# Two buffers for the dense experts' gate tile, three instead of four for v's two parts

## The chip, the cores and the metric

One core of a Trainium2 chip runs the whole kernel. The metric is the device time of one execution in microseconds, the median over runs. TensorE (PE; its weight loads are PEld) does the matmuls, VectorE (DVE), ScalarE (ACT) and GpSimd (POOL) the rest, and SyncE (SP) issues most of the DMAs.

## What is computed

One block of an encoder on 1024 tokens of width 1024 in float32: a mixer (differential attention and a short convolution, gated and summed), then PEER, a retrieval over 128 x 128 experts of one neuron each, then a final norm. The change touches PEER alone:

```python
q = (xc @ w_query).reshape(c, PEER_HEADS, 2, PEER_HALF_DIM)
sc = jnp.einsum('chpd,hpnd->chpn', q, sub_keys)
s1, i1 = lax.top_k(sc[:, :, 0], PEER_TOPK); s2, i2 = lax.top_k(sc[:, :, 1], PEER_TOPK)
top, pos = lax.top_k(cand, PEER_TOPK)          # cand: sums of s1 and s2
g = jax.nn.softmax(top, axis=-1)
u = expert_u[eidx]
a = jax.nn.gelu(jnp.einsum('chkd,cd->chk', u, xc), approximate=False)
vv = expert_v[eidx]
out = jnp.einsum('chk,chkd->cd', g * a, vv)    # 8 heads x 16 experts of each token
```

## The kernel before, in words

The tokens are eight tiles of 128. The kernel computes PEER in two ways at once. For five tiles (640 tokens, "dense") it runs over all 16384 experts and multiplies by a gate that is zero for experts that were not chosen. For the other three tiles it gathers each token's 128 chosen experts from HBM.

**The dense part** (the loop at the end of `block_kernel`) takes the experts in 128 groups of 128; the text calls such a group an expert. `expert_in(i)` loads the group's rows of u (`raw`, three buffers, shared with v), splits them in two parts (`uh` by a cast on ACT, the remainder `uhl` on DVE), makes z = u h in 48 matmuls of 320 columns (two column halves, eight steps of K, three products of parts each), takes Gelu on ACT into `pr`, multiplies `pr` by the gates on DVE (line 930) and splits the product in `ph` and `phl`. `expert_v(i)` loads the rows of v and splits them in `vh` (ACT) and `vhl` (DVE), with `VHB` buffers of each. `expert_out` takes a block of two experts at once and adds their products to ten tiles of output (five token tiles, two halves of the width): four of them stay in PSUM (`held`), six go through `pout` and are added to `hacc` on DVE (line 957). Half of the ten tiles are done in each of two iterations, after `expert_in` and before `expert_v`. So both experts' `vh` and `vhl` are read until the second of these iterations is over; there are 30 matmuls of 512 columns in an iteration.

**The gates.** The weights of all experts for the dense tokens lie in HBM (`w_d`), written before this stage. Line 920 loads those of four experts at a time (`WB`) into `wt`, 1280 KB, in runs of 512 bytes, issued by SyncE; 32 such loads in all. Four multiplications of line 930 read one load. `wt`'s pool `dn` has room for one.

**The gathers** run beside it: POOL fetches one expert's u and v for each of 128 tokens by indirect DMA (1 MB, line 739) into `uvt` (four buffers); DVE takes the product with h (line 746), ACT Gelu and the gate (748, 749; this small tile is named `wt` as well), DVE adds v times that to `acc` (line 755). There are 384 of them. A generator hands out their instructions in step with the estimated time of the dense matmuls. The choice of experts for these tokens runs on DVE in the first part of the stage.

**Order.** The kernel is written in a tile language; buffers with the same tag rotate, and a tile waits until a buffer of its tag is free. The program is built with `tile.TileContext(nc, schedule_with_timeline_sim=True)`: the order of instructions on each engine is planned at build time along a simulated timeline and is then fixed, so it need not be the order of the code. Each engine, and SyncE's issuing, goes through its own list in order. A change of the number of buffers can change the plan.

Of the kernel before, what the change touches and what calls it, by code (L numbers as in the profile page):

```python
# [10 lines left out]
F32 = mybir.dt.float32  # L11
# [9 lines left out]
P = 128  # L21
# [6 lines left out]
GB = NB * P  # L28
# [15 lines left out]

UVT = 4
PHB = 4
VHB = 4
BLK = 2
NR = 2
WB = 4  # L50
WT = 32
# [14 lines left out]
def block_kernel(ctx, tc, x, wqkv, wcols, wpr, wo, wq, skT, uv, uT, an_w, fn_w, fin_w, sub_w,  # L66
# [7 lines left out]
    def pool(name, bufs=1, stack=None, **kw):  # L74
        return (stack or left).enter_context(tc.tile_pool(name=name, bufs=bufs, **kw))
# [382 lines left out]
    def halves(n):  # L458
        return [(0, n)] if n <= 512 else [(0, n // 2), (n // 2, n // 2)]
# [428 lines left out]
    du, dn, dv, hp, gat = (pool(n) for n in ("du", "dn", "dv", "hp", "gat"))  # L888
# [4 lines left out]
    def split(t, tag, bufs, shape, eng):  # L893
        pl = du if tag == "uh" else dv
        hi = pl.tile(shape, F32R, name=tag, tag=tag, bufs=bufs)
        A.copy(out=hi, in_=t)  # L896
        lo = pl.tile(shape, F32R, name=f"{tag}l", tag=f"{tag}l", bufs=bufs)
        eng.tensor_sub(lo, t, hi.bitcast(F32))  # L898
        return hi, lo

    def passes(ps, lhs, rhs, cols, first=True, last=True):
        n = len(lhs)
        for k in range(n):
            for j, (a, b) in enumerate(((0, 0), (0, 1), (1, 0))):
                PE.matmul(ps, lhsT=lhs[k][a], rhs=rhs[k][b],  # L905
                          start=first and k == 0 and j == 0, stop=last and k == n - 1 and j == 2)
        tick(cols / 2400 * 3 * n)

    wts = {}

    def raw_rows(src):
        t = du.tile([P, D], F32, name="raw", tag="raw", bufs=3)
        SP.dma_start(out=t, in_=src)
        return t

    def expert_in(i):
        b = i // WB
        if i % WB == 0:
            wts[b] = dn.tile([P, GB // WT, WB, WT], F32, name="wt", tag="wt", bufs=1)
            SP.dma_start(out=wts[b], in_=w_d[:, :, i:i + WB, :].rearrange("c p i t -> p c i t"))  # L920
        ur = raw_rows(uT[i])
        u = split(ur, "uh", 2, [P, D], V)
        us = [(u[0][:, k * P:(k + 1) * P], u[1][:, k * P:(k + 1) * P]) for k in range(KD)]
        hs = halves(GB)
        z = ps_z.tile([P, 2, 512], F32, name="z", tag="z")[:, :len(hs), :hs[0][1]]
        for j, (c0, cn) in enumerate(hs):
            passes(z[:, j, :], us, [(hh[:, k, c0:c0 + cn], hl[:, k, c0:c0 + cn]) for k in range(KD)], cn)
        p = dn.tile([P, GB], F32, name="pr", tag="pr", bufs=1)
        A.activation(p.rearrange("p (h c) -> p h c", h=len(hs)), z, AF.Gelu)  # L929
        V.tensor_mul(p.rearrange("p (c t) -> p c t", t=WT), p.rearrange("p (c t) -> p c t", t=WT),  # L930
                     wts[b][:, :, i % WB, :])
        return split(p, "ph", PHB, [P, GB], V)

    def expert_v(i):
        vr = raw_rows(uv[i * P:(i + 1) * P, D:])
        return split(vr, "vh", VHB, [P, D], V)

# [36 lines left out]
    for i in range(NK + BLK):  # L974
        if i < NK:
            pv.append(expert_in(i))
        b, part = i // BLK - 1, i % BLK
        if b >= 0:
            expert_out(pv[:BLK], vv[:BLK], part, b == 0, b == NK // BLK - 1)
            if part == BLK - 1:  # L980
                pv, vv = pv[BLK:], vv[BLK:]
        if i < NK:
            vv.append(expert_v(i))
        if i == 1:
            for t in range(NR, NB):
                SP.dma_start(out=hacc[:, t - NR, :], in_=h_d[t * P:(t + 1) * P, :])
# [56 lines left out]
```

## Time and profile before

| | |
|---|---|
| median of 3 runs | 3235.85 us (3223.81 to 3254.53) |
| the profiled execution | 3236.47 us, its span 3234.7 us |
| mean granted clock of TensorE over the span | 0.973 |
| dense stage | from about 1316 us to the end |

The profile is of one execution. A row of a stretch gives each engine's busy time and number of instructions, the granted clock as a share of full speed, the share of time that the 16 DMA engines were busy, and what they moved. A row of waits gives who waited, for whom, the sum in us, how often and the longest. A row of the timeline gives start and duration in us, the engine, line and operation, what is written and read, and in brackets how long the engine was idle before it and what ended that. Matmuls overlap in the pipeline, so their own durations are longer than their spacing.

### The profile page before, as it was taken

Reading aid. Unit: us, or ns where it says so; the run is one execution under the profiler, and the core shown is the slowest. Engines: PE = TensorE matmul, PEld = TensorE weight load, DVE = VectorE, ACT = ScalarE, POOL = GpSimd, SP = SyncE. Lnnn points to the kernel's source line nnn. Section 1 sums busy time; section 2 is a strip of 40 time slices with the busy share of each in tenths; the row PEclk is TensorE's granted clock in tenths of the full one; section 3 lists DMA queues with packets and bytes.
Section 4 is the critical chain, followed back from the end, with each engine's and each line's share of the span. In section 5 each row is a group of like instructions: output and inputs, shape, how many; then the busy total and the mean of one; then the engine's idle time right before and its main releaser. Section 6 shows DMA issues by size and latency. Waiting matters only on the chain.

```text
span 3234.7 us, 46047 instructions
## 1 busy us (share of the span) xinstructions
PE 3017.4 (93%) x17551; PEld 2768.1 (86%) x17551; DVE 2647.0 (82%) x4665; ACT 1298.3 (40%) x2344; POOL 954.6 (30%) x716
## 2 busy tenths in 40 slices
PE   7999999898999889799999999999999999999992
PEld 6799988798888779798989989889888999998891
DVE  4442565478999996798999999999999999998898
ACT  3322464335567757433333333333333333333332
POOL 2310000045444444232223323322333323233333
PEclk9999999999999989899999999999999999999996
DMA  5451232555444374787888888878789899988997
GB/s 177 146 177 66 82 111 92 211 164 202 146 177 182 148 269 161 265 297 274 304 291 293 308 286 315 323 275 316 268 301 339 325 348 338 339 329 317 327 331 288
DMA packets 237550, 801.12 MB, mean 248 GB/s; under 512 B 18832, under 2 KB 123280, under 8 KB 174096
## 3 DMA queue, kind: packets, MB, share of 16 engines
q0 software_dynamic: 64704, 442.53, 37.4%
q1 hardware_dynamic: 152592, 305.30, 27.2%
q10 hardware_dynamic: 20032, 50.34, 4.1%
q8 instruction: 138, 2.26, 0.3%
q14 instruction: 84, 0.69, 0.1%
HBM read 714.74 MB, written 83.36 MB: 247 GB/s over the span
## 4 chain that ended last, share of the span: by engine, by line
PE 36%; DVE 20%; issue 18%; DMA 15%; POOL 7%; ACT 3%; SPq 0%; POOLq 0%; ACTq 0%; DVEq 0%
DMA wt<-w_d 7%; PE z L905 7%; POOL uvt L739 6%; PE pg L228 4%; DMA uvt<-in_uv,idx 4%; PE pq L228 4%; PE pout L905 4%; DVE acc L755 3%; PE ph L228 3%; DVE uvt L746 3%; PE held L905 2%; PE py L228 2%; PE pw L695 2%; DVE hacc L957 2%; PE pv L228 1%
## 5 line engine op out<-in xcount | busy, mean ns | idle before, releaser
L739 POOL DMA_INDIRECT uvt<-in_uv,idx x384 | 552.6, 1439 | 1297.0 <-DVE acc L755 852.8
L905 PE MATMUL z<-actTh,uh 128*128 128x320 f32 x2048 | 636.7, 311 | 2.1 <-ACT pr L929 1.1
L905 PE MATMUL z<-actTh,uhl 128*128 128x320 f32 x2048 | 637.6, 311 | 0.0
L905 PE MATMUL z<-actTl,uh 128*128 128x320 f32 x2048 | 636.1, 311 | 0.0
L746 DVE SCALAR_TENSOR_TENSOR uvt<-uvt,hng 128x1024 f32<-128x1024 f32 x384 | 472.7, 1231 | 48.6 <-DMA uvt<-in_uv,idx 42.9
L755 DVE SCALAR_TENSOR_TENSOR acc<-uvt,wt,acc 128x1024 f32<-128x1024 f32 x381 | 486.4, 1277 | 6.1 <-ACT wt L749 4.8
L905 PEld LDWEIGHTS z<-actTh,uh 128*128 128x128 f32 x2048 | 387.1, 189 | 12.2 <-ACT pr L929 2.1
L905 PEld LDWEIGHTS z<-actTl,uh 128*128 128x128 f32 x2048 | 387.4, 189 | 8.8
L905 PEld LDWEIGHTS z<-actTh,uhl 128*128 128x128 f32 x2048 | 387.9, 189 | 4.0
L905 PE MATMUL pout<-vh,ph 128*128 128x512 f32 x768 | 306.5, 399 | 47.0 <-DVE hacc L957 30.2
L748 ACT ACTIVATE wt<-zt 128x1 f32<-128x1 f32 x384 | 77.5, 202 | 668.4 <-DVE uvt L746 667.5
L905 PE MATMUL pout<-vhl,ph 128*128 128x512 f32 x768 | 302.7, 394 | 0.0
L905 PE MATMUL pout<-vh,phl 128*128 128x512 f32 x768 | 301.9, 393 | 0.6 <-DVE phl L898 0.6
L718 POOL TENSOR_TENSOR o<-ms,wtr 128x512 f32<-128x512 bf16 x160 | 204.7, 1322 | 256.5 <-PE pw L695 127.3
L957 DVE TENSOR_TENSOR hacc<-pout,hacc 128x512 f32<-128x512 f32 x384 | 260.5, 681 | 2.8 <-PE pout L905 2.8
L185 DVE TENSOR_TENSOR wl<-wr,wh 128x2048 fp32r<-128x2048 f32 x66 | 157.2, 2382 | 118.8 <-ACT wh L184 114.7
L896 ACT CAST ph<-pr 128x640 fp32r<-128x640 f32 x128 | 93.3, 729 | 394.2 <-DVE pr L930 394.2
L905 PEld LDWEIGHTS pout<-vh,ph 128*128 128x128 f32 x768 | 145.7, 190 | 78.7 <-DVE hacc L957 39.5
L695 PE MATMUL pw<-o,o 128*128 128x128 f32 x1280 | 172.3, 288 | 39.8 <-POOL o L718 20.2
L184 ACT CAST wh<-wr 128x2048 fp32r<-128x2048 f32 x74 | 141.1, 1909 | 168.8 <-DMA wr<-in_wq 41.5
L695 PEld LDWEIGHTS pw<-o,o 128*128 128x128 f32 x1280 | 164.3, 201 | 47.7 <-POOL o L718 26.9
L905 PE MATMUL held<-vh,ph 128*128 128x512 f32 x512 | 200.6, 392 | 0.7 <-ACT ph L896 0.7
(290 smaller groups left out, 6760.4 us busy)
## 6 DMA issues: line engine op xcount, KB each, us to landing
raw<-in_uT SPq DMA_DIRECT2D x128, 512.0 KB, 6.5
raw<-in_uv SPq DMA_DIRECT2D x128, 512.0 KB, 8.0
w_d<-wbuf ACTq DMA_DIRECT2D x20, 2048.0 KB, 7.0
wt<-w_d SPq DMA_DIRECT2D x32, 1280.0 KB, 16.0
wr<-in_wcols SPq DMA_DIRECT2D x28, 1024.0 KB, 5.1
wr<-in_wq SPq DMA_DIRECT2D x24, 1024.0 KB, 5.2
xt<-in_x SPq DMA_DIRECT2D x16, 512.0 KB, 4.0
q_d<-qt POOLq DMA_DIRECT2D x32, 256.0 KB, 3.5
```

The costliest lines, as they stand in the source:

```text
L184: A.copy(out=op[0][sl], in_=src)
L185: lo.tensor_sub(op[1][sl], src, op[0][sl].bitcast(F32))
L228: PE.matmul(pd, lhsT=l[a], rhs=r[b], start=i == 0 and j == 0, stop=i == n - 1 and j == len(c) - 1)
L695: PE.matmul(pw[:, u, :], lhsT=o2[:, t + u, :], rhs=o1[:, t + u, :], start=True, stop=True)
L718: PL.tensor_tensor(out=o1.rearrange("p t i -> p i t"), in0=ms[:, 0], in1=w[:, ts].unsqueeze(1).broadcast_to(sh), op=ALU.mult)
L739: PL.indirect_dma_start(out=t[:], out_offset=None, in_=uv, in_offset=bass.IndirectOffsetOnAxis(ap=sels[c][1][:, k:k + 1], axis=0))
L746: V.scalar_tensor_tensor(u, u, 1.0, st[c], op0=ALU.mult, op1=ALU.mult, accum_out=zt)
L748: A.activation(wt, zt, AF.Gelu)
L755: V.scalar_tensor_tensor(st["acc"], v, wt, st["acc"], op0=ALU.mult, op1=ALU.add)
L896: A.copy(out=hi, in_=t)
L905: PE.matmul(ps, lhsT=lhs[k][a], rhs=rhs[k][b], start=first and k == 0 and j == 0, stop=last and k == n - 1 and j == 2)
L957: V.tensor_add(hacc[:, t - NR, ds], ps, hacc[:, t - NR, ds])
```

## The change

`VHB` goes from 4 to 3: `vh` and `vhl` each have three buffers of 4 KB a partition instead of four. The gate tile `wt` has two buffers instead of one, of 10 KB a partition each. Nothing else is edited; the number of instructions and the bytes moved are the same.

```diff
-VHB = 4
+VHB = 3
@@ expert_in(i)
         if i % WB == 0:
-            wts[b] = dn.tile([P, GB // WT, WB, WT], F32, name="wt", tag="wt", bufs=1)
+            wts[b] = dn.tile([P, GB // WT, WB, WT], F32, name="wt", tag="wt", bufs=2)
             SP.dma_start(out=wts[b], in_=w_d[:, :, i:i + WB, :].rearrange("c p i t -> p c i t"))
```

## Rows read from the trace of the kernel before

**Rows 1.** The page: busy us, share of the span, instructions.
```profile
PE 3017.4 (93%) x17551; PEld 2768.1 (86%) x17551; DVE 2647.0 (82%) x4665; ACT 1298.3 (40%) x2344; POOL 954.6 (30%) x716
```

**Rows 2.** Stretches: us, busy PE, PEld, DVE, ACT, POOL, PEclk, DMA share, GB/s.
```profile
1400.00:1600.00 200.00, 193.43 (x1067) 175.43 (x1066) 184.71 (x313) 66.07 (x133) 60.51 (x39) 0.98 0.81 288
...
2000.00:2200.00 200.00, 192.02 (x1056) 173.62 (x1055) 185.48 (x314) 66.43 (x132) 57.44 (x40) 0.98 0.84 301
...
2600.00:2800.00 200.00, 200.00 (x1121) 182.78 (x1121) 185.97 (x236) 71.13 (x149) 57.99 (x45) 1.00 0.94 342
```

**Rows 3.** DVE's waits, 1350 to 3160 us: sum, times, longest.
```profile
DVE pr L930 <- DMA wt<-w_d: 80.7, 23, 8.4
```

**Rows 4.** Timeline of one late load: SyncE, then DVE, then PE.
```profile
1493.18 0.38 SPq L920 DMA_DIRECT2D wt<-w_d  x1
...
1515.63 0.82 DVE L930 TENSOR_TENSOR pr<-pr,wt 128x640 f32<-128x640 f32 x1 [8.36 <-DMA wt<-w_d]
...
1518.26 0.80 PE L905 MATMUL pout<-vh,ph 128*128 128x512 f32 x1 [5.29 <-DVE hacc L957]
```

**Rows 5.** The tile wt: its loads (issue, ns), and their times to landing.
```profile
L920 SPq DMA_DIRECT2D wt<-w_d x32: 377/377/537, 1326.0 to 3103.8; - x32
...
DMA to landing us min/median/max: 9.1/16.0/22.7
```

**Rows 6.** PE's waits, 1350 to 3160 us.
```profile
PE pout L905 <- DVE hacc L957: 26.1, 20, 5.3
PE held L905 <- DVE phl L898: 5.4, 4, 4.2
```

**Rows 7.** PE's waits after a load: stretches 1452 to 1459 and 3063 to 3070.
```profile
PE pout L905 <- DVE hacc L957: 1.2, 1, 1.2
...
PE pout L905 <- DVE hacc L957: 2.2, 1, 2.2
```

**Rows 8.** Start of the stage: PE's first output matmul; a stretch before it.
```profile
1347.72 0.79 PE L905 MATMUL pout<-vh,ph 128*128 128x512 f32 x1 [16.57 <-ACT ph L896]
...
1336.00:1346.00 10.00, 0.00 (x0) 0.00 (x0) 0.00 (x0) 0.00 (x0) 0.00 (x0) 0.50 1.03 402
```

**Rows 9.** ACT's waits for vh; timeline of first, last and worst of them.
```profile
ACT vh L896 <- PE pout L905: 56.0, 29, 4.7
...
1409.90 1.05 ACT L896 CAST vh<-raw 128x1024 fp32r<-128x1024 f32 x1 [1.19 <-PE pout L905]
...
1414.13 1.21 DVE L898 TENSOR_TENSOR vhl<-raw,vh 128x1024 fp32r<-128x1024 f32 x1
...
3133.64 1.05 ACT L896 CAST vh<-raw 128x1024 fp32r<-128x1024 f32 x1 [0.96 <-PE pout L905]
...
3137.25 2.35 DVE L898 TENSOR_TENSOR vhl<-raw,vh 128x1024 fp32r<-128x1024 f32 x2
...
2340.52 2.00 ACT L896 CAST vh<-raw 128x1024 fp32r<-128x1024 f32 x2 [1.51 <-PE pout L905]
...
2349.48 2.35 DVE L898 TENSOR_TENSOR vhl<-raw,vh 128x1024 fp32r<-128x1024 f32 x2
```

**Rows 10.** Timeline of PE: a matmul of z, and the one five later.
```profile
2643.72 0.31 PE L905 MATMUL z<-actTl,uh 128*128 128x320 f32 x1
...
2644.45 0.40 PE L905 MATMUL pout<-vh,ph 128*128 128x512 f32 x1
```

**Rows 11.** SyncE's waits at raw loads, 1340 to 3210 us.
```profile
SPq L913 <- DVE uhl L898: 588.9, 118, 14.2
```

**Rows 12.** Timeline of the end: PE's last matmul, then gathers on DVE.
```profile
3177.18 0.40 PE L905 MATMUL pout<-vh,phl 128*128 128x512 f32 x1
...
3205.66 1.29 DVE L755 SCALAR_TENSOR_TENSOR acc<-uvt,wt,acc 128x1024 f32<-128x1024 f32 x1 [0.60 <-ACT wt L749]
...
3223.21 1.22 DVE L746 SCALAR_TENSOR_TENSOR uvt<-uvt,hng 128x1024 f32<-128x1024 f32 x1
...
3225.04 1.28 DVE L755 SCALAR_TENSOR_TENSOR acc<-uvt,wt,acc 128x1024 f32<-128x1024 f32 x1 [0.60 <-ACT wt L749]
```

## The prediction

> **What bounds the kernel now.** I read the page's busy times first, then the table of stretches, then who waited for whom on DVE and PE, then single stalls in the timeline. Over the span PE is 93% busy and DVE 82% [rows 1]. The change touches only the dense-expert stage, from about 1316 us to the end, so I read that stage alone. There PE is busy 193.4 us of a 200 us stretch early on and all 200 later, with DVE at 184 to 186 beside it [rows 2]: PE sets the pace, DVE has some 7% to spare, and a DVE that comes late is what makes PE wait. The last matmul starts at 3177.2 us [rows 12]; from there to the span's end, some 57 us, gathers and closing norms are left.
>
> DVE's largest wait in this stage is the multiplication by the gates, line 930, which waits for the load of wt: 80.7 us in 23 waits between 1350 and 3160 us [rows 3]. One of them shows why. The load is issued at 1493.18 us, when the multiplication before it has given wt's only buffer back; it lands 22.4 us later; DVE runs dry for 8.36 us; PE then waits 5.29 us for an hacc that DVE could not add in time [rows 4]. There are 32 such loads, one in four experts, of 9.1 to 22.7 us, median 16.0 [rows 5]; an expert takes about 14 us, so the load is usually late by a few us.
>
> **What the stall is worth to PE.** PE's waits for DVE between 1350 and 3160 us are 26.1 us for hacc and 5.4 us for phl [rows 6]. Of the 32 loads, 11 are followed within about 14 us by PE waits: 1.2, 5.3, 2.6, 1.3, 0.3, 2.5, 3.1, 1.9, 0.4, 1.9 and 2.2 us, together 22.7 us; the first and the last of the 11 stand in [rows 7]. So of DVE's 80.7 us PE feels 22.7, a bit over a quarter. The rest DVE's own slack swallows.
>
> **The change, part by part.**
>
> *Second wt buffer.* Instructions added: none; the same 32 loads and 128 multiplications. The load for block b+1 needs the buffer of block b-1, free a whole block earlier, some 55 us (31 intervals from 1326.0 to 3103.8 us are 57.3 us each [rows 5]). SyncE, which issues it, may then stand at a raw load in front of it, at most 14.2 us [rows 11], and the longest landing was 22.7 us [rows 5]: 57 - 14 - 23 leaves 20 us. The wait goes whole: -22.7 us on PE. Bounds: 0 if something else is late at the same place, -31.5 us if all of PE's waits for DVE go. What is late next on DVE: nothing of that size (its other waits for gathers are already there).
>
> *Clock.* After PE's gaps the granted clock shows below 1: 0.98 in 1400-1600 and in 2000-2200 us, 1.00 in the full stretch [rows 2]. The levels being 1.2 and 2.4 GHz, 0.98 means 4% of the time at half speed, so 2% of 200 us = 4 us lost in each. I take back 5 of these 8 us, about the share of the waits that goes (bounds 0 and 8).
>
> *Start of the stage.* PE waits 16.57 us at 1347.72 for the first wt [rows 8]. This stays; and now the second load can be issued right behind the first, while the DMA engines are full (402 GB/s, share 1.03 [rows 8]). Its 1.31 MB at 402 GB/s is 3.3 us: +3 (bounds 0, if it is issued later, and 3.3).
>
> *Three vh buffers.* Two experts are a block; both of its vh are held until the second half of the block's output is done on PE. With four buffers the next pair can be cast while the old one is read. With three only the first of the next pair can; the second waits for PE's last matmul of the block, and is wanted after the z of one expert. The cover is 48 matmuls, 0.146 us apart [rows 10], 7.0 us; three passes with the pair's first expert follow, so I take 7.5 us. Against this stands the time from PE's release to the end of vhl. Before has it too, where a cast waits for PE: 29 times, 56.0 us [rows 9]. Read one by one (cast on ACT, subtraction on DVE) they take 5.4 us in the first, 4.9 in the last, 10.2 in the worst [rows 9]; the mean is 5.1, and two exceed 7.5 us, by 0.5 and 2.7. That is 3.2 us in 29, 0.11 each; 64 pairs give +7 us. Bounds: 0 if the planner lets PE do other tiles first, and +56 if each came 3 us later (below).
>
> Behind a cast that waits at the head of ACT stand the gather's two small activations and the Gelu of z. ACT's waits for PE before vh are 1.9 us each (56.0 / 29) [rows 9]; 35 more (64 pairs less 29) would be 67 us of ACT, which is 40% busy [rows 1]. I put nothing for it: ACT was idle for 56.0 us in just this place without a PE wait that is put down to vh [rows 6, 9]. The other bound is a rival below.
>
> *Sum.* The profiled execution took 3236.5 us (span 3234.7 and 1.8 around it); the median shown is 3235.9, so I go by the former. 3236.5 - 22.7 - 5 + 3 + 7 = 3218.8; I say 3219.
>
> The order of instructions on each engine is planned anew when the program is built, so other waits may move; the rivals below are where that could decide.
>
> **Rivals.**
>
> *The gathers give the gain back.* The gather stream has four buffers and passes DVE in order. Late in the stage a gather starts every 4.44 us (45 in 200 us [rows 2]). If that pace does not follow a faster PE, PE ending 18 us sooner leaves 4 more gathers for the tail, where one takes 3.23 us (six steps from 3205.66 to 3225.04 us [rows 12]): +13, so 3232. For it: the tail is gathers alone. Against it: they start when DVE gives a buffer back, and DVE is what becomes faster.
>
> *DVE's free time goes into gathers.* The 80.7 us less the 22.7 leave 58 us of DVE. A use of a gather costs it 1.22 + 1.28 us [rows 12], so up to 23 could be done earlier; after PE's last matmul 14 such additions remain, the last at 3225.04 us [rows 12], 45 us at 3.23. Were ten of them pulled forward, 32 us: 3187. For it: a gather starts only when DVE gives a buffer back. Against it: DVE's order is fixed, and a wait that vanishes does not itself put another gather before the end of the dense part.
>
> *The other side: the second vh comes late.* One mechanism: at the end of a block ACT and DVE get two splits of v at once, one urgent, and the urgent vhl stands behind the other or behind a uhl (1.2 us each) and an addition. With the 29 latencies shifted by 2 us the excess over 7.5 us is 0.35 us a pair, 22 us in 64 pairs: from there on the gain is gone. At 3 us it is 0.87, 56 us: 3236.5 - 22.7 - 5 + 3 + 56 = 3268. Against it: DVE is itself less late once it no longer stalls.
>
> *Work queued behind the cast.* If the 67 us of ACT reach DVE and, by the ratio of 22.7 to 80.7, a quarter of that PE, it is 19 us more: 3238. For it: DVE needs ACT for each gather, with 93% of its time taken [rows 2]. Against it: PE showed nothing of the first 56 us [rows 6, 9]. The Trainium skill, "TensorE: Matmul & The Clock Gate", section "Architectural detail: the array is 16× 32×32, not 1× 128×128", has the rule behind this rival: ScalarE and VectorE take their queues strictly first in, first out. By it those 19 us are owed and no gain is left; the trace agrees on the order, and not so far on the price.
>
> *It does not do what it says.* If the planner put the load late in SyncE's queue the stall would remain: 3236.5 + 7 = 3244. The 20 us of margin speak against it.
>
> **How the numbers follow.** My forecast 0.43; gathers give it back 0.12; work behind the cast 0.07; gathers pulled forward 0.18; vh late 0.17; no effect 0.03. What a measurement of this kernel can tell from no change is about 1%, 32 us: 3203.5 to 3268 is "same". Faster: the pulled gathers and a sixth of the forecast, 0.26. Slower: most of the late vh and the tail of the forecast, 0.19. Same: the rest, 0.55. The range runs from the pulled gathers to the late vh with a tenth left out at each end, 3185 to 3264; the likeliest case alone 3205 to 3232.
>
> **What would show it.** Right: no DVE wait for wt after the first block, the loads issued some 50 us before use; PE's waits for hacc down by two thirds; the last matmul near 3158 us; a tail of some 57 us; the first PE wait 17 to 20 us. For vh: ACT's waits for PE before a cast rise to about 64, PE's waits for vh or vhl sum to under 10 us. Wrong: PE waits for vhl of tens of us, a tail that is longer or shorter by more than 15 us, or a stage whose PE time does not shrink although the wt wait is gone.

## The result, and the profile after

The changed kernel takes 3192.39 us (median of 4 runs, 3184.85 to 3204.41) against 3232.65 us of four runs of the kernel before: a ratio of 0.986, interval 0.9825 to 0.9896. That is 1.4% less (the two medians alone give 1.2%), and the interval leaves no change out. The profiled execution took 3191.8 us, 44.7 less than that of before; the forecast was 17.7 less.

The stage table shows in which part the 44.7 us went. Three stretches of the kernel after (columns as in [rows 2]), then its dense stage up to PE's end (the end of its last matmul) and what follows it, the tail:

```profile
1400.00:1600.00 200.00, 198.55 (x1104) 179.56 (x1103) 196.36 (x329) 69.04 (x140) 56.17 (x41) 1.00 0.85 307
...
2000.00:2200.00 200.00, 198.59 (x1100) 179.28 (x1099) 191.19 (x326) 69.17 (x138) 59.70 (x41) 1.00 0.86 307
...
2600.00:2800.00 200.00, 200.00 (x1121) 182.67 (x1120) 184.30 (x233) 72.00 (x149) 62.12 (x44) 1.00 0.90 334
...
1318.00:3148.46 1830.46, 1799.12 (x9984) 1629.17 (x9982) 1723.46 (x2604) 628.03 (x1289) 543.72 (x392) 1.00 0.88 319
3148.46:3190.00 41.54, 0.00 (x0) 0.00 (x0) 30.61 (x39) 8.92 (x26) 12.80 (x11) 0.55 0.72 266
```

The same two stretches of before:

```profile
1318.00:3177.58 1859.58, 1804.58 (x9970) 1634.87 (x9969) 1711.17 (x2591) 619.68 (x1277) 567.74 (x387) 0.99 0.86 311
3177.58:3234.70 57.12, 0.00 (x0) 0.00 (x0) 41.42 (x53) 11.49 (x36) 17.85 (x16) 0.53 0.74 276
```

PE ends 29.1 us sooner (3177.6 to 3148.5), and the tail behind it is 15.6 us shorter (57.1 to 41.5). Against [rows 2], PE's early stretches went from 193.4 and 192.0 us of 200 to 198.6, and the clock there from 0.98 to 1.00. The tail is shorter because fewer gathers are left in it: DVE has 39 instructions there instead of 53, and of the gather additions (line 755) 9 instead of 14. DVE goes through its list in a fixed order, so this number is set when the program is built: in that list 13 gather additions stand behind the last addition to hacc (line 957) before, and 8 after.

DVE's column gives the other account of the same 44.7 us. From 1318 us to the span's end DVE is busy 1711.2 + 41.4 = 1752.6 us before and 1723.5 + 30.6 = 1754.1 us after: the same work. What fell is its idle time, from 1916.7 - 1752.6 = 164.1 us to 1872.0 - 1754.1 = 117.9 us, by 46.

The load that the change meant to hide is hidden. The tile wt and its loads (columns as in [rows 5]), and DVE's wait for it:

```profile
L920 SPq DMA_DIRECT2D wt<-w_d x32: 377/377/3456, 1328.1 to 3015.6; - x32
...
  DMA wt<-w_d: 10.4, 1
```

Of the 24 waits of the whole stage (91.5 us; [rows 3] has 23 of them) only the first is left, 10.4 us. The last load is issued at 3015.6 us, not at 3103.8 [rows 5].

DVE's, PE's and ACT's waits of the kernel after (sum, times, longest), DVE and PE from 1350 to 3131 us:

```profile
DVE uvt L746 <- DMA uvt<-in_uv,idx: 36.6, 35, 4.0
DVE hacc L957 <- PE pout L905: 19.1, 27, 2.2
DVE pr L930 <- ACT pr L929: 17.7, 17, 3.1
DVE uhl L898 <- ACT uh L896: 13.2, 7, 5.6
...
PE pout L905 <- ACT ph L896: 15.0, 1, 15.0
PE pout L905 <- DVE hacc L957: 4.7, 7, 1.3
PE z L905 <- ACT pr L929: 2.2, 4, 0.9
PE held L905 <- ACT vh L896: 1.2, 4, 0.4
PE z L905 <- DVE uhl L898: 1.1, 3, 0.6
...
ACT pr L929 <- PE z L905: 204.6, 78, 8.2
ACT uh L896 <- DMA raw<-in_uT: 187.9, 79, 8.3
ACT vh L896 <- PE pout L905: 115.7, 46, 7.4
```

The first line of PE is the start of the stage. Behind it PE waits 9.9 us in all, where before it waited 33.1, of that 26.1 for hacc [rows 6]. DVE's wait for gathers is as before (37.4). The three DVE lines under it are new or larger; these are the same waits of before, with two of ACT's:

```profile
DVE hacc L957 <- PE pout L905: 2.8, 3, 1.7
DVE uhl L898 <- ACT uh L896: 2.6, 4, 1.3
...
ACT uh L896 <- DMA raw<-in_uT: 22.7, 11, 4.7
ACT pr L929 <- PE z L905: 10.1, 7, 2.7
```

So 81 us of DVE's wait for wt went (91.5 less 10.4), and 45 us came back in three places: hacc +16.3, the Gelu before pr +17.7, uhl +10.6. DVE's other waits fell by some 11 us together, the larger parts of it a wait for the tile hng (5.5 to 0.4) and those of the gathers for ACT (4.8 to 1.2). That makes the 46.

The Gelu's lateness is PE's: before 16 of these 17 waits ACT itself stood idle until PE had finished z. One of them (start and duration in us, idle time before):

```profile
2650.13 0.71 ACT L929 ACTIVATE pr<-z 128x640 f32<-128x640 f32 x1 [5.01 <-PE z L905]
...
2650.87 0.83 DVE L930 TENSOR_TENSOR pr<-pr,wt 128x640 f32<-128x640 f32 x1 [3.08 <-ACT pr L929]
```

So two of the three new waits, hacc and the Gelu, are DVE waiting for PE. Only the first part of the change was meant to take the wait for wt away; which of the two parts brought how much of the time is a matter for the experiments.

### The profile page after: what moved, and what is told of

It reads as the page before. It is cut to its first block, busy times and chain, and to the rows that moved or that the text cites. A ratio compares the mean times of both kernels' runs of the same rounds, so it can differ in the third digit from the quotient of the medians.

```text
span 3190.0 us, 45907 instructions
## 1 busy us (share of the span) xinstructions
PE 3012.1 (94%) x17551; PEld 2761.0 (87%) x17551; DVE 2646.3 (83%) x4665; ACT 1302.9 (41%) x2344; POOL 923.5 (29%) x716
## 4 chain that ended last, share of the span: by engine, by line
PE 56%; DVE 17%; issue 11%; DMA 8%; POOL 4%; ACT 3%; SPq 0%; ACTq 0%; POOLq 0%; DVEq 0%
PE z L905 17%; PE pout L905 10%; PE held L905 6%; PE pq L228 4%; PE pg L228 4%; POOL uvt L739 3%; PE ph L228 3%; DMA uvt<-in_uv,idx 3%; DVE acc L755 2%; PE py L228 2%; PE pw L695 2%; DVE uvt L746 2%; DVE ms L714 1%; PE pv L228 1%; PE pk L228 1%
## 5 line engine op out<-in xcount | busy, mean ns | idle before, releaser
L739 POOL DMA_INDIRECT uvt<-in_uv,idx x384 | 528.1, 1375 | 1288.5 <-DVE acc L755 1011.0
L755 DVE SCALAR_TENSOR_TENSOR acc<-uvt,wt,acc 128x1024 f32<-128x1024 f32 x381 | 487.8, 1280 | 1.3 <-ACT wt L749 1.2
L905 PE MATMUL pout<-vh,ph 128*128 128x512 f32 x768 | 302.5, 394 | 23.2 <-ACT ph L896 15.0
L896 ACT CAST uh<-raw 128x1024 fp32r<-128x1024 f32 x128 | 134.3, 1049 | 193.5 <-DMA raw<-in_uT 187.9
L905 PE MATMUL held<-vhl,ph 128*128 128x512 f32 x512 | 199.6, 391 | 0.0
L720 ACT CAST o<-ms 128x512 f32<-128x512 bf16 x160 | 179.6, 1138 | 38.8 <-DVE ms L714 26.0
```

The lines of the kernel that those rows point to most:

```text
L720: A.copy(out=o2.rearrange("p t i -> p i t"), in_=ms[:, 1])
L739: PL.indirect_dma_start(out=t[:], out_offset=None, in_=uv, in_offset=bass.IndirectOffsetOnAxis(ap=sels[c][1][:, k:k + 1], axis=0))
L755: V.scalar_tensor_tensor(st["acc"], v, wt, st["acc"], op0=ALU.mult, op1=ALU.add)
L905: PE.matmul(ps, lhsT=lhs[k][a], rhs=rhs[k][b], start=first and k == 0 and j == 0, stop=last and k == n - 1 and j == 2)
```

## The experiments

For each, "PE's end" and "tail" are of its profiled execution as above, "DVE idle" is from 1318 us to the span's end, and the ratio is to runs of the kernel before on the same chip.

| kernel | median us | ratio, interval | PE's end | tail | gathers in it | DVE busy / idle |
|---|---|---|---|---|---|---|
| before | 3232.7 | | 3177.6 | 57.1 | 14 | 1752.6 / 164.1 |
| after | 3192.4 | 0.986 (0.9825 to 0.9896) | 3148.5 | 41.5 | 9 | 1754.1 / 117.9 |
| vh3_alone | 3209.9 | 0.9936 (0.9912 to 0.9959) | 3177.6 | 38.9 | 8 | 1750.2 / 148.3 |
| wt2_small | 3237.7 | 1.002 (1.0004 to 1.0036) | 3120.7 | 112.5 | 32 | 1752.7 / 162.5 |
| wt2_ph3 | 3215.7 | 0.9948 (0.993 to 0.9967) | 3161.3 | 48.3 | 10 | 1753.3 / 138.3 |
| vh2_wt2 | 3305.0 | 1.0236 (1.02 to 1.0272) | 3282.4 | 14.2 | 0 | 1756.7 / 221.9 |
| wb2_vh3 | 3235.5 | 0.9986 (0.9966 to 1.0006) | 3126.3 | 106.3 | 30 | 1757.5 / 157.1 |
| wb2_vh3_uvt5 | 3190.9 | 0.985 (0.9817 to 0.9884) | 3163.2 | 27.1 | 5 | 1749.6 / 122.7 |
| after_g16 | 3193.7 | 0.9854 (0.9819 to 0.9889) | 3158.3 | 42.4 | 9 | 1755.5 / 127.2 |
| gather120 | 3190.9 | 0.9836 (0.9794 to 0.9877) | 3182.8 | 13.6 | 0 | 1694.2 / 184.2 |
| ph3_alone | 3247.2 | 1.0012 (0.9988 to 1.0036) | 3213.4 | 52.6 | 13 | 1756.5 / 191.5 |
| ph5_alone | 3242.6 | 1.0003 (0.9978 to 1.0028) | 3172.2 | 56.7 | 14 | 1750.6 / 160.3 |
| wt2_vh3_ph3_uvt5 | 3202.3 | 0.9888 (0.9849 to 0.9927) | 3190.2 | 14.2 | 0 | 1752.8 / 133.6 |
| uhl_pool | 3206.0 | 0.9878 (0.9853 to 0.9902) | 3189.9 | 15.6 | 0 | 1808.9 / 78.6 |

The medians come from several chips, on which the kernel before took 3231 to 3245 us, so rows of different chips are compared by their ratios. The profiled executions of ph3_alone, after_g16 and gather120 are the longest of their runs (ph3_alone's by 21 us over its median) and that of vh3_alone is 8 us over its median, so their PE's end and idle time are some us high; that of vh2_wt2 is the shortest of its four. The medians go before them. Through the whole table the tail is about 14 us, for the closing norms, and some 3 us for each gather left in it.

**vh3_alone**: the second part of the change without the first.

```diff
-VHB = 4
+VHB = 3
```

> One part alone: three buffers for vh and vhl, the gate tile still with one. Theory A (the late load of wt is what the change removed): the DVE wait for wt stays near 80 us between 1350 and 3160 us and the time is that of the kernel before plus a small price of the third buffer, 0 to 10 us, so 3232 to 3245. Theory B (the gain comes from the new plan that three vh buffers bring, other orders on PE and DVE): a good part of the 40 us is here already, under 3215. Theory C (three buffers are dear, and the second wt buffer had to pay for it first): 3250 or more.

Measured: 0.64% less time, the case of theory B. The stage and the tail, then waits, then PE's first output matmul:

```profile
1318.00:3177.60 1859.60, 1812.13 (x9984) 1634.90 (x9983) 1721.20 (x2604) 627.25 (x1288) 558.24 (x392) 0.99 0.86 313
3177.60:3216.50 38.90, 0.00 (x0) 0.00 (x0) 28.98 (x38) 8.50 (x24) 10.65 (x10) 0.55 0.72 265
...
DVE pr L930 <- DMA wt<-w_d: 69.9, 19, 8.6
PE pout L905 <- DVE hacc L957: 21.6, 16, 4.3
PE z L905 <- DVE uhl L898: 9.4, 7, 2.9
...
ACT uh L896 <- DMA raw<-in_uT: 172.9, 72, 9.2
...
1338.03 0.50 PE L905 MATMUL pout<-vh,ph 128*128 128x512 f32 x1 [1.03 <-ACT ph L896]
```

PE's end does not move at all, and DVE still waits 69.9 us for wt; yet the tail has lost 18.2 us and six gathers. So the shorter tail belongs to the plan that comes with three vh buffers, not to the free time of the second gate buffer: behind the last addition to hacc DVE's list has 7 gather additions here, 13 before. By medians the change splits into about 21 us for the one part (3231.2 beside it, less 3209.9) and 17.5 us for the other (3209.9 less 3192.4), by ratios into 0.64% and 0.76%, so into halves as far as the runs can tell; by profiles into the tail (-18.2, then +2.6) and PE's end (0, then -29.1).

That PE's end stands still is a sum of two things. PE's first output matmul comes 9.7 us sooner than in [rows 8], since the first wait there, 16.57 us, is 1.03 here; from it to its end PE takes 9.6 us more (1839.5 for 1829.9), with waits for uhl that before does not have.

**wt2_small**: the first part without the second. There was no room for two whole gate tiles with four vh buffers, so each tile holds two experts; the loads are smaller too, and no run has small tiles with a single buffer.

```diff
-WB = 4
+WB = 2
...
-            wts[b] = dn.tile([P, GB // WT, WB, WT], F32, name="wt", tag="wt", bufs=1)
+            wts[b] = dn.tile([P, GB // WT, WB, WT], F32, name="wt", tag="wt", bufs=2)
```

> Double buffering without touching vh: the gate tile holds two experts instead of four, with two buffers of 5 KB, the same room as one of 10 KB; VHB stays 4. The loads are 64 of 640 KB in runs of 256 bytes instead of 512. Theory A: the DVE wait for wt goes, the time is that of the changed kernel or some us less, 3180 to 3197, unless the shorter runs slow the DMA engines. Theory B: with the old number of vh buffers little is gained, 3220 to 3240. Theory C: clearly below the changed kernel, 3175 or less, as no price of vh is paid.

Measured: no gain, as theory B had it, though every wait for wt but the first is gone. Its late stretch, stage and tail:

```profile
2600.00:2800.00 200.00, 200.00 (x1119) 182.62 (x1118) 173.55 (x222) 68.17 (x139) 50.70 (x39) 1.00 0.89 312
...
1318.00:3120.70 1802.70, 1784.33 (x9941) 1626.71 (x9939) 1667.66 (x2535) 610.24 (x1242) 515.74 (x369) 1.00 0.89 309
3120.70:3233.20 112.50, 0.01 (x1) 0.00 (x0) 85.05 (x106) 19.95 (x70) 46.78 (x33) 0.52 0.83 307
```

PE ends 56.9 us sooner than before and the tail is 55.4 us longer. Between 1350 and 3110 us PE waits only 0.2 us; DVE, which has lost all but 6.9 us of its waits for wt, is now held up by uhl, whose cast waits for PE:

```profile
DVE uhl L898 <- ACT uh L896: 80.7, 47, 4.4
...
ACT uh L896 <- PE z L905: 308.1, 103, 6.8
```

DVE is busy 173.6 us in this late stretch, not the 186.0 of [rows 2], with 38 gathers started on GpSimd where there were 44 (its 39 and 45 instructions have one of another kind each). A stall that is taken from DVE does not go to the gathers by itself: in this plan 31 gather additions stand behind the last addition to hacc, and the stall's time went to a faster PE alone.

**wt2_ph3**: two whole gate tiles with four vh buffers, the room taken from ph; and **ph3_alone**, its control.

```diff
-PHB = 4
+PHB = 3
```

> The second gate buffer with vh left at four; the room is taken from ph and phl instead, three buffers of each for four. Theory A: no DVE wait for wt, 3180 to 3200; ACT's waits for PE before vh fall back to about 29. Theory B: 3220 to 3240. Theory C: below 3180, or, should ph be as dear as vh, near the changed kernel with PE waiting for ph.

> The kernel before with three buffers of ph and phl instead of four; vh and the gate tile as before. Theory E (a split with fewer buffers can run less far ahead, so the planner gives DVE to the gathers sooner and fewer are left at the end): as with three vh buffers alone, 8 to 11 gathers left after PE's last matmul instead of 14, a tail of 39 to 50 us, 3210 to 3228. Theory F (three vh buffers gained their 21 us by the chance of one plan): the number left goes either way, and the time stays within 10 us of the kernel before or above it.

Measured: three ph buffers alone change nothing (1.0012). With them the second gate buffer brings 0.52% against before, between theories A and B, and 0.64% against ph3_alone by the two ratios, some 21 us; on top of three vh buffers it is 0.76% or 25 us by the ratios and 17.5 us by the medians. The intervals of these differences are 0.3 to 0.4% wide to each side. DVE's wait for gathers has grown in wt2_ph3, and PE waits for hacc and phl:

```profile
DVE uvt L746 <- DMA uvt<-in_uv,idx: 81.7, 64, 4.4
PE pout L905 <- DVE hacc L957: 14.5, 9, 2.7
PE pout L905 <- DVE phl L898: 7.9, 7, 2.2
```

ph3_alone has 91.3 us in 58 of these waits for gathers, so those belong to the plan with three ph buffers. The second gate buffer is worth some 20 us in two plans and nothing in the one of wt2_small.

**vh2_wt2**: after, with the disputed cover of v taken away altogether.

```diff
-VHB = 3
+VHB = 2
```

> The changed kernel with two vh buffers for three: both experts of the next block must wait for the end of the block that PE is at, so both splits, 2 x 1.05 us on ACT and 2 x 1.2 us on DVE, stand against the 7 us of one z. Theory A and my price for vh (latency from release to vhl, mean 5.1 us, against a cover of 7.5): the second vhl comes 1.5 to 3 us after the first, so 0.5 to 2 us a pair, 64 pairs: 30 to 130 us over the changed kernel, 3222 to 3320. If the planner can fill PE with other tiles meanwhile, as Theory B has it, under 10 us over the changed kernel.

Measured: 3.8% more than after (1.0236 / 0.986). All gathers are done when PE ends, but it ends at 3282.4 us. PE's waits:

```profile
PE pout L905 <- DVE hacc L957: 41.5, 23, 5.0
PE z L905 <- DVE uhl L898: 19.5, 18, 3.2
PE pout L905 <- DVE vhl L898: 18.2, 21, 3.6
```

So there is a price for vh buffers that are taken away, clear of noise when two are. Even here PE's waits for vhl itself are the smaller part; most come by hacc and uhl, from a DVE that is late (221.9 us idle).

**wb2_vh3** and **wb2_vh3_uvt5**: the long tail of wt2_small attacked from two sides, with three vh buffers, then with a fifth buffer for the gathered rows too.

```diff
-UVT = 4
+UVT = 5
```

> The changed kernel with the gate tile halved: two experts a load, two buffers of 5 KB, three vh buffers. It is the control of the next run. Theory D (the time is PE's end plus a tail of the gathers that are left; the gathers go round their four buffers, so their pace is the length of that round divided by four): PE ends near 3125 as in the kernel with small gate tiles and four vh buffers, the tail is long, 60 to 110 us, 3200 to 3235. Theory A (the DVE wait for wt is all that counts): 3180 to 3197.

> The same with five gather buffers instead of four, in the room that the halved gate tile leaves. Theory D: a round of some 20 us over five buffers instead of four, a gather every 4.2 us where it was 5.2, so all gathers are done within the dense part and the tail falls to 15 to 25 us; DVE then has all of its work before PE's end, which moves to 3130 to 3155; 3150 to 3175. Theory A: no change against the control.

Measured: three vh buffers move two gathers here, not six, and the time stays (0.9986). The fifth gather buffer moves 25 more and gives 44.6 us (3235.5 to 3190.9): tail 106.3 to 27.1, PE's end 3126.3 to 3163.2. It comes out level with after. The 3150 to 3175 of theory D was missed: PE ends 8 us or more later than it said, and five gathers are left. DVE's largest wait is then for the Gelu:

```profile
DVE pr L930 <- ACT pr L929: 83.2, 43, 4.8
```

**after_g16**: does the rate at which the program hands out gathers among the experts set the tail?

```diff
-GATHER = 2.0
+GATHER = 1.6
```

> The changed kernel with the gathers handed out faster in the program's order (GATHER 1.6 us of estimated matmul time a step instead of 2.0). Theory D: their buffers set the pace and not the hand-out, so the period of a gather stays near 5.1, 4.75 and 4.55 us in the three thirds and the time within 8 us of the changed kernel. If instead the hand-out sets the pace, the tail shrinks from 42 to some 15 to 20 us and the time is 3165 to 3180.

Measured: 0.9854, as after; 9 gathers in the tail, and as many in each expert as in after, as theory D had it. The hand-out rate does not set the pace; the buffers do, as the two runs with five of them show (30 gathers left become 5, and 9 become none).

**gather120**: before, with eight of each token's 128 experts not gathered.

```diff
-            for k in range(NE):
+            for k in range(NE - 8):
```

> The kernel before with 120 gathers instead of 128 for each of the three tiles (the last eight experts of each token are left out): 24 gathers of 1 MB less. It measures what a gather that is left over costs. Theory D: the 14 gathers after PE's last matmul go, the tail falls from 57 to some 15 us, DVE's waits for wt and PE's end stay within 15 us: 3185 to 3200. If the tail were set by the closing norms and stores, it stays above 40 us and the time above 3215.

Measured: 1.64% less. Nothing is changed at wt, and its wait is the same as in [rows 3]; PE's end is 5 us later; the whole gain is the tail (57.1 to 13.6 us), as theory D had it. The stage and the wait:

```profile
1318.00:3182.80 1864.80, 1805.07 (x9969) 1634.04 (x9967) 1689.09 (x2562) 620.12 (x1262) 555.21 (x375) 0.99 0.84 304
...
DVE pr L930 <- DMA wt<-w_d: 80.4, 23, 9.0
```

DVE has 58 us less to do (1752.6 to 1694.2), and the tail is 43.5 us shorter. The tail is left-over DVE work on gathers, and can be had without touching PE.

**ph5_alone**: I had come to suspect that a smaller buffer count moves the plan in one direction, and a larger one in the other.

```diff
-PHB = 4
+PHB = 5
```

> The same with five buffers of ph and phl. Theory E: the dense splits run further ahead, 16 gathers or more are left, a tail of 60 us or more, 3240 to 3260. Theory F: no order with the number of buffers; a tail near or under 57 us is as likely.

Measured: 1.0003, 14 gathers in the tail. DVE's list has as many gathers in each expert as before, so the fifth buffer left the plan of the gathers as it was. With 13 gathers left by three ph buffers, where theory E had 8 to 11, no such order is seen. Why three vh buffers leave six gathers fewer with the one large gate tile and two fewer with the small ones stays open.

**wt2_vh3_ph3_uvt5**: can all gathers be done by the time PE ends, without PE ending later?

```diff
-PHB = 4
+PHB = 3
-UVT = 4
+UVT = 5
```

> The changed kernel with the room for a fifth gather buffer taken from ph and phl (three instead of four); the gate tile stays at four experts, two buffers. Theory D (the round of the gather buffers sets their pace, and what is left at the end makes the tail): the period falls below 4.7 us, at most 4 gathers are left, the tail is 14 to 27 us; PE pays up to 15 us for ph, as with three of ph and two gate buffers, and ends between 3150 and 3165: 3165 to 3190, below the changed kernel. If the DMA engines, 0.90 busy late in the stage, are what paces the gathers, the tail stays above 35 us and the time at 3190 to 3205.

Measured: no. The tail is down to 14.2 us without a gather, but PE's end is 41.7 us later than in after, and the kernel is no faster (0.9888 against 0.986, with intervals that overlap):

```profile
PE pout L905 <- DVE hacc L957: 34.6, 22, 3.3
```

PE waits 34.6 us for hacc again. DVE's work is the same 1752.8 us; it is only done in another place. That a gather which is pulled before PE's end stands on DVE in front of an hacc is argued: three ph buffers came with it, and their share is not separated.

**uhl_pool**: then the time must fall if DVE's work does. After, with every second uhl (64 of 128) subtracted on GpSimd.

```diff
-        u = split(ur, "uh", 2, [P, D], V)
+        u = split(ur, "uh", 2, [P, D], PL if i % 2 else V)
```

> The changed kernel with the subtraction for uhl of every second expert on GpSimd instead of DVE: 64 of 1.25 us, 80 us, leave DVE; on GpSimd they take some 2.3 us each (half of its 4.67 us for twice the size), 150 us where it is 30% busy. Theory G (DVE's work, 1750 to 1757 us from 1318 us on in every run so far but the one with fewer gathers, plus its idle time is what makes the length; the wait for wt was 91 us of that idle time): with 80 us less work the time falls by 40 to 80 us, to 3115 to 3155, unless the idle time grows by as much. If PE sets the pace and DVE's share does not matter, PE ends near 3145 and the time stays at 3180 to 3195. GpSimd also issues the gathers, in order; if these come late behind the subtractions, DVE's wait for gathers grows above 60 us and eats the gain.

Measured: no faster than after (0.9878 of before, against 0.986), so theory G's 3115 to 3155 was missed. DVE's work did not fall by 64 x 1.25 = 80 us, it rose by 55 (1754.1 to 1808.9). DVE groups of uhl_pool with the GpSimd one, then the DVE groups of after (count, busy, mean ns, idle before):

```profile
L755 DVE SCALAR_TENSOR_TENSOR acc<-uvt,wt,acc 128x1024 f32<-128x1024 f32 x381 | 542.2, 1423 | 12.2 <-ACT wt L749 12.0
...
L957 DVE TENSOR_TENSOR hacc<-pout,hacc 128x512 f32<-128x512 f32 x384 | 261.4, 685 | 5.1 <-PE pout L905 4.9
...
L898 POOL TENSOR_TENSOR uhl<-raw,uh 128x1024 fp32r<-128x1024 f32 x64 | 170.4, 2662 | 78.1 <-ACT uh L896 63.7 <-DVE tk L590 5.5 <-PE pout L905 4.7
```

```profile
L755 DVE SCALAR_TENSOR_TENSOR acc<-uvt,wt,acc 128x1024 f32<-128x1024 f32 x381 | 487.8, 1280 | 1.3 <-ACT wt L749 1.2
...
L957 DVE TENSOR_TENSOR hacc<-pout,hacc 128x512 f32<-128x512 f32 x384 | 259.4, 681 | 19.6 <-PE pout L905 19.1
```

DVE's idle time is the lowest of all, 78.6 us, and still the kernel is not faster: the 39 us that it saved in idle against after went into 55 us of slower work (see the last section). So this run does not test what less work on DVE is worth; gather120 is the one run in which it fell.

## Why the prediction was right or wrong

The time fell inside the range, 3185 to 3264, but under the likeliest case's own 3205 to 3232, and on the side, faster by over 1%, to which I gave 0.26. The forecast of 3219 was 27 us too long. That it fell inside owes something to luck: the range's low edge stood for a mechanism, gathers pulled forward by DVE's freed time, that the runs do not show.

**The step that failed is the tail, held at some 57 us, with the time taken as PE's end plus that constant.** It is 41.5 us in the changed kernel and 13.6 to 112.5 us over all runs. Gathers that the plan puts behind the dense part in DVE's list come after PE's end at about 3.1 us each, so a PE that ends sooner is worth nothing in itself (wt2_small: 57 us sooner, 55 us of tail). That PE sets the pace holds in the dense part, where DVE's new waits are for PE; but the 7% that DVE seemed to have to spare there was not spare, as what it does not do there it does after PE's end. DVE's work is 1750 to 1758 us in every kernel that does all of it on DVE and without GpSimd's subtractions, whatever the time. The span is that work, DVE's idle time, and the 1318 us before: 1318 + 1752.6 + 164.1 = 3234.7. Such a sum holds for any engine by definition; what the runs add is that its middle term stays the same. I added up PE's waits only; a sum in DVE's idle time would have had the tail in it.

**Second gate buffer: right in what it does, and its worth near the sum in part by luck.** The loads are issued 59 to 78 us ahead of their use (I said some 50), and no wait for wt is left after the first block. PE's waits behind the start fell by 23.2 us (33.1 to 9.9), where I had 22.7, and those for hacc from 26.1 to 4.7 us, by more than the two thirds I named. But of 81 us of DVE's wait, 45 came back as waits for PE, the Gelu and uhl. I wrote that nothing of that size would be late next on DVE; that was wrong. What the part is worth in time hangs on the plan that it meets: some 20 us on top of three vh or three ph buffers, and none in wt2_small, where PE gained most. The sum had no term for that.

**Three vh buffers: sign wrong in the time.** I put +7 us on PE. After shows 1.2 us of PE's waits for vh and none for vhl; vh3_alone shows 0.3 us for vhl and 9.4 for uhl, and PE's 9.6 us more from its first output matmul on, of the size that I named but no larger than what executions differ by. ACT's waits for PE before a cast rose from 56.0 us in 29 to 115.7 in 46, where I had said 64 times, about 120 us, for all pairs. Alone the part gives 21 us less, through the order in which the plan puts the gathers. The prediction's one sentence on that, that the order is planned anew and other waits may move, had no number, and this was about half of the gain. Something is paid elsewhere: ACT's uh waits for raw loads rise from 22.7 us to 172.9 in vh3_alone, which changes no other count, and to 187.9 in after. That rows of v which can't be split yet stay in raw is the likely way and is argued; no run changed raw alone.

**Clock: twice what I gave it.** Expected -5, with bounds 0 and 8. From PE's first output matmul to its end the granted clock is 0.50, the lower of its two levels (1.2 and 2.4 GHz), for 27 us in six places before, and after for the first 4 us alone. One of the six, which begins within PE's gap of 5.29 us in [rows 4], and the rest of the stage after:

```profile
1515.00:1522.00 7.00, 3.74 (x10) 3.16 (x11) 6.37 (x11) 1.72 (x5) 0.00 (x0) 0.51 0.23 92
...
1354.00:3148.46 1794.46, 1780.49 (x9879) 1611.92 (x9878) 1705.25 (x2548) 617.91 (x1278) 538.90 (x388) 1.00 0.88 318
```

Half of that time is 13.7 us lost before and 2.1 after, so some 11.6 came back. I had read two stretches only, and there are falls at 1635, 3068 and 3171 us beside those at 1515 and 2130. With 23 us of waits that is more than the 31.2 us by which this part of PE's work became shorter (1829.9 to 1798.7); some 4 us of wider spacing stand against it.

**Start.** Expected +3: the first z starts 2.0 us later, the second load is issued at 1334.18 us, 6 us behind the first, but PE's first wait is 15.0 us and not 17 to 20. The first output matmul comes 2.0 us later, so this small term held.

**PE's last matmul** was to be near 3158 us and is at 3148.1: the clock gave more back, and the +7 did not come.

**Rivals.** *DVE's free time goes into gathers* (0.18, 3187) came nearest in its number, but its mechanism fell: of the ten gathers five moved, and vh3_alone moves six with the wait for wt at 69.9 us. *The gathers give the gain back* (0.12) did not happen in the change, where 9 gathers are left and not 18; it happened whole in wt2_small. What I held against it, that gathers start when DVE gives a buffer back and DVE gets faster, is not enough: DVE's order is fixed, so its freed time passes to what stands next in it. Its pace of 4.44 us counted 45 GpSimd instructions, of which 44 are gathers. *The second vh comes late* (0.17): PE's waits for vhl are 0.3 us in vh3_alone and 18.2 in vh2_wt2, so it needs one buffer less. *Work queued behind the cast* (0.07): ACT's waits for PE before vh rose by 59.7 us, but DVE's new waits for the Gelu come from PE's z and not from that queue, and its waits for the gathers' ACT work fell; on PE the waits for the Gelu and uhl come to 2.2 + 1.1 us, not 19. *It does not do what it says* is excluded: one wait for wt of 10.4 us is left.

**What the prediction said would show it wrong** was among other things a tail that differs by more than 15 us. It differs by 15.6.

## What to carry to other kernels

Where two engines are both above 90% busy, take the span as one engine's work plus its idle time for each of the two, to the very end with the tail; a gain on one counts only as far as it shortens the other's idle time too. Ask of each stall that is removed what stands next on the engine that had it: here 81 us of waits made room for 45 us of others, and in one plan the whole gain was handed to the tail. When a program orders its instructions by a plan made from buffer counts, a change of one count can also be a new order: three vh buffers brought 21 us that way, three ph buffers another order and no gain, five ph buffers no other order of the gathers. Each count needs its own run, alone.

## What the runs showed of the hardware that was not expected

DVE's instructions with two inputs in SBUF became longer while GpSimd subtracted. Beside the 64 subtractions, acc's mean went from 1280 to 1423 ns and vhl's from 1227 to 1457, while hacc, one of whose inputs is in PSUM, stayed at 681 to 685 ns. Two vhl of the same shape in uhl_pool's timeline (start us, duration us), and the GpSimd instruction beside the second:

```profile
2310.61 1.22 DVE L898 TENSOR_TENSOR vhl<-raw,vh 128x1024 fp32r<-128x1024 f32 x1
...
2312.89 3.42 DVE L898 TENSOR_TENSOR vhl<-raw,vh 128x1024 fp32r<-128x1024 f32 x1
...
2312.14 3.08 POOL L898 TENSOR_TENSOR uhl<-raw,uh 128x1024 fp32r<-128x1024 f32 x1 [1.24 <-ACT uh L896]
```

The second ends at 2316.31 us; GpSimd's ends at 2315.22, and 1.22 us after that would be 2316.44. It looks as if DVE did its work only when GpSimd had finished. The whole stage says the same: 13 vhl that start while such a subtraction runs take 2.88 us on average and end 1.0 us after it, 104 vhl with none beside them take 1.23, and 4 hacc that start in the same way keep their 0.69. In sum 170.4 us of GpSimd took 80 us off DVE and put about 135 on it (1808.9 less 1754.1 plus 80).

The Trainium skill, "SBUF — State Buffer", section "Who interferes with whom", says that DVE and GpSimd share one pair of SBUF ports as an exclusive lock, and that nothing else among the engines contends; the section adds that a DVE instruction with two SBUF inputs asks for this pair against a GpSimd instruction that reads SBUF. The trace agrees for these two engines, in the 3.42 us and in hacc's unchanged 685 ns.
